# First loads in another order, two more pairs of y tiles for product 5, one query tile for all heads

## Chip, core and metric

The kernel runs on one core of a Trainium2 chip. The metric is the device time of one execution in microseconds (us). The core has five engines that run side by side, each through its own queue in order: PE (matrix products, with its weight loads shown as PEld), ACT, DVE, POOL, and SP, which issues most of the transfers (DMAs). A DMA from SP or POOL goes to the same 16 DMA engines.

## The reference, cut to what matters

Two layers over 1024 latent tokens and 256 context tokens, each of width 1024. Each layer takes a root-mean-square norm of its input, scales and shifts it by a modulation worked out from a conditioning vector, projects it, mixes tokens, and projects back with a gate:

```
def _ada(cvec, w, b):
    m = jax.nn.silu(cvec) @ w + b
    return jnp.split(m.reshape((-1, 1, m.shape[-1])), 3, axis=-1)
...
for l in range(DEPTH):
    shift, scale, gate = _ada(c, w_ada[l], b_ada[l])
    h_lat = _rms(x, norm_w[l]) * (1.0 + scale) + shift
    h_ctx = _rms(ctx, norm_w[l]) * (1.0 + scale_c) + shift_c
    ...   # layer 0: neighbourhood attention beside mLSTM heads; layer 1: 16 HGRN2 heads
    x = x + gate * y_lat
```

Layer 1 (`_c_mixer`) runs for each of 16 heads a gated recurrence in both directions, with query `q`, a decay `f` and key `1 - f` per direction, and ends in an output projection of a 2048 x 1024 weight matrix.

## The kernel before

All arithmetic is float32. A float32 product is split: each operand becomes a high part (`hi`, a cast on ACT, L73) and a low part (`lo`, the difference, on DVE, L74), and three matmuls `hi*hi`, `hi*lo`, `lo*hi` (L131 to L133) make one product. So each weight block and each activation tile is first a raw tile that a DMA fills, and then a pair of tiles.

Tiles come from pools. A tile is asked for under a tag; a tag has a number of buffers, and a further request for the tag gets a buffer when all uses of its earlier tile are over. The order of the instructions on each engine and on SP is not the program's order: a planner lays them out beforehand, by priority (the program's order, with helpers that make some steps urgent and others fillers) and by its own estimate of when each is ready. `issue_after(ins)` puts what a block issues behind `ins` on the queue of `ins`.

Three places matter here.

**The first loads** (from L1293). `load_x` (L1298) loads one 128 x 1024 tile of x and norms it: a square with a sum on ACT (L237), a reciprocal root on POOL (L157, L159), a scaling on DVE (L239). `gate_cols` (L280) loads 272 columns of the first weight matrix, "value weights" (`wvr`), and splits them into `wvh` and `wvl`. `ada` (L186, `ada_rows` L168) loads the modulation weights in eight chunks of 1 MB (`adar`, three buffers), multiplies each on PE (L177), and at the end copies the row (`adarow`, L192), turns it and writes the modulation; its last instruction is `mod_done` (L208). Then, in pairs of tiles, `mod_tr` (L242) transposes x on PE (L251), applies the modulation on ACT and DVE (`ntmp`, L259, L261) and splits the result into `hh` and `hl` (L274, L275); `values_gates` (L292) multiplies these with the value weights. The order of the loads is: two x tiles, value weights, modulation chunks, the other eight x tiles. x tiles have six buffers.

**The heads of layer 1** (L1443). `hg_intra` of a head writes the query tile `gQ` in four pieces (L1038): for the upper half of the tokens (`hf` = 1) and then the lower half, for both directions. Seven levels follow, each a set of small matmuls on PE (L1059, `strip`) and updates of `gQ` and `gK` on DVE (L1106). `hg_scan` (L1119) goes through eight chunks of 128 tokens in rising order; its matmuls at L1138 and L1139 read `gQ`, chunk by chunk, and its state update is `gS` on DVE (L1144). `gQ` has one buffer and is asked for anew in each head.

**The output projection** (from L1463). It is done as seven smaller products over halves of rows and columns. `y_block` (L1504) loads a 128 x 512 tile of the activations and splits it into `yh` and `yl`. For product 5 (weights `w5`, results `m5`), the tiles y of k = 0 to 3 are made early; then k = 4 to 6 (L1614) are loaded, split and used one by one, and k = 7 (`y7`) follows. `later` is a list of weight loads, and `loads()` (L1556) starts the next. `final` (L1548) writes one result tile `og` (four buffers) and adds it into the output in memory with a DMA from POOL; `f2` (L1563) is its use for four tiles just before product 5. `product` (L1589) does products 6, 3 and 4, and `f4` (L1580) writes the last four tiles with plain DMAs from SP.

Of the kernel before, what the change touches and what calls it, by code (L numbers as in the profile page):

```python
# [10 lines left out]
F32 = mybir.dt.float32  # L11
F32R = mybir.dt.float32r
# [7 lines left out]
P = 128  # L20
D = 1024
KD = D // P
LAT = 1024
# [22 lines left out]
class Prog:  # L46
# [980 lines left out]
    def hg_intra(self, h, st, pool):  # L1027
        nc = self.nc
        F, q = st["F"], st["q"]
        K = self.t(pool, [P, 2, LAT], F32, "gK", 1)  # L1030
        nc.vector.tensor_scalar(out=K, in0=F, scalar1=-1.0, scalar2=1.0, op0=ALU.mult, op1=ALU.add)
        Q = self.t(pool, [P, 2, LAT], F32, "gQ", 1)
        ks = [self.t(pool, [P, 512], F32, "gkn", 4) for _ in range(2)]
        for hf in (1, 0):
            s = slice(hf * 512, (hf + 1) * 512)
            nc.vector.tensor_tensor(out=ks[hf], in0=K[:, 0, s], in1=K[:, 1, s], op=ALU.add)
            for d in range(2):
                nc.vector.tensor_tensor(out=Q[:, 1 - d, s], in0=q[hf], in1=F[:, d, s], op=ALU.mult)  # L1038
        hv = dict(Q=Q, K=K, T=F, D=self.t(pool, [P, 8, 64], F32, "gD", 1))
        hv["A"] = self.t(pool, [P, 8, P], F32, "gA", 1)  # L1040
        if h == 0:
            self.t(pool, [P, 16], F32, "pad", 1)
        pa = self.ps("s", [P, 8, 64])
        with self.urgent():
            for c in range(8):
                for b in range(2):
                    o = c % 4 * P + b * 64
                    self.strip(pa[:, c, :], b, ks[c // 4][:, o : o + 64], q[c // 4][:, o : o + 64])
        nc.vector.tensor_tensor(
            out=hv["D"], in0=pa, in1=self.lmask[:, 0, :].unsqueeze(1).to_broadcast([P, 8, 64]), op=ALU.mult  # L1050
        )
        for lev in range(7):
            self.hg_level(hv, lev, pool)
        return hv
# [23 lines left out]
    def hg_level(self, H, lev, pool):  # L1078
        nc = self.nc
        n, h = LAT, 1 << lev  # L1080
        nb = n // (2 * h)
        K, Q, A, D, Tt = H["K"], H["Q"], H["A"], H["D"], H["T"]

        pick = lambda t: _skew(t[:, 0, :].rearrange("p (b s i) -> p b s i", s=2, i=h), 2, n)
        out = self.ps("s", [P, 8, 64])
        with self.urgent():
# [5 lines left out]
            for c in range(8):  # L1092
                for b in range(2):
                    o = c * P + b * 64
                    r = out[:, c, :]
                    if lev < 6:
                        r = r.rearrange("p (b s i) -> p b s i", s=2, i=h)
                        lhsT, rhs = ksel[:, o : o + 64], pick(Q)[:, o // (2 * h) : (o + 64) // (2 * h)]
                    else:
                        lhsT = K[:, b, o : o + 64]  # L1100
                        rhs = Q[:, 1 - b, c * P + (1 - b) * 64 : c * P + (2 - b) * 64]
                    self.strip(r, b, lhsT, rhs)
            for t, o, step in ((Q, n + 1, -n - 1), (K, 1, n - 1)):
                v = bass.AP(t.tensor, t.offset, [list(t.ap[0]), [n + h, 2], [2 * h, nb], [1, h]])
# [106 lines left out]
    def build(self):  # L1211
        tc, nc, a = self.tc, self.nc, self.a
        dma = nc.sync.dma_start
        with ExitStack() as es:
# [78 lines left out]
            with self.pp.phase(ad=1), tc.tile_pool(name="pre", bufs=2) as pool:  # L1293
                self.adab = 3
                self.wide_c(pool)
                xts = {}

                def load_x(tt):  # L1298
                    xts[tt] = self.t(pool, [P, D], F32, "x0", 6)
                    self.last_dma = dma(out=xts[tt], in_=self.xin(tt))  # L1300
                    self.norm(xts[tt], xts[tt], pool)

                for tt in range(2):
                    load_x(tt)
                wv = self.gate_cols(pool)
                with tc.issue_after(self.last_dma.ins):
                    for step in self.ada(0, pool, nc.sync):
                        step()
                mod_pair = lambda tt: self.mod_tr(0, [xts[tt], xts[tt + 1]], tt, pool, self.h_sink(tt * P))
                with tc.issue_after(self.last_dma.ins), tc.issue_after(self.mod_done.ins):  # L1310
                    for tt in range(2, NT):
                        if tt % 2 == 0:
                            mod_pair(tt - 2)
                        load_x(tt)
                x_dma = self.last_dma
                mod_pair(NT - 2)
                self.values_gates(wv)
# [35 lines left out]
            with tc.tile_pool(name="ml", bufs=2) as pool, self.pp.phase(s=2, acc=2):  # L1353
# [22 lines left out]
                yp = wr.enter_context(tc.tile_pool(name="oy", bufs=1, side="right"))  # L1376
# [8 lines left out]
            with tc.tile_pool(name="op0", bufs=2) as op, ExitStack() as wl:  # L1385
# [3 lines left out]
                raws = [yp, 3, "woraw"]  # L1389
# [46 lines left out]
            with l1:  # L1436
                pool = l1.enter_context(tc.tile_pool(name="hg", bufs=2))
# [5 lines left out]
                for h in range(16):  # L1443
# [7 lines left out]
                    if h == 15:  # L1451
                        rh.close()
                        yp = es.enter_context(tc.tile_pool(name="oy", bufs=1, side="right"))
# [19 lines left out]
                def add(out, x, y, op=ALU.add):  # L1473
                    nc.vector.tensor_tensor(out=out, in0=x, in1=y, op=op)
# [21 lines left out]
                for t in range(4):  # L1496
# [4 lines left out]
                    hi, lo = self.out_y(t, 1, y2, yp, 4, ks=((0, 4), (4, 3)))  # L1501
                    self.dense(m2[t], lambda i: hi[i], lambda i: lo[i], w2.h, w2.l, 7, True, False)

                def y_block(src, k, raws):  # L1504
                    yh, yl = [self.t(yp, [P, 512], F32R, "y" + c, 4) for c in "hl"]
                    yr = self.t(*raws)
                    dma(out=yr, in_=src(k))
                    self.split(yh, yl, yr)
                    return yh, yl

                def block_mm(ps, t, y, w, k, n):
                    at = slice(t * P, (t + 1) * P)
                    self.dense(
                        ps, lambda i: y[0][:, at], lambda i: y[1][:, at], lambda i: w.h(k), lambda i: w.l(k),
                        1, k == 0, k == n - 1,
                    )

                later, r16 = [], []
                w5 = block(self.sw[0], _Late(wr * 4, r16), later)
# [3 lines left out]
                w5_dma = self.last_dma  # L1523
                m5 = [self.ps("c", [P, 512]) for _ in range(2)]
                y5 = [y_block(lambda k: self.s5[k], k, (yp, [P, 512], F32, "wraw", self.yraws)) for k in range(4)]
                for k in range(4):
                    for t in range(2):
# [7 lines left out]
            with tc.tile_pool(name="op1", bufs=2) as op, ExitStack() as wl, tc.issue_after(w5_dma.ins):  # L1535
# [6 lines left out]
                for b in range(2):  # L1542
                    g = self.t(op, [P, 512], F32, f"gbc{b}", 1)
# [3 lines left out]

                def final(tt, b, x, y, op_=ALU.add):  # L1548
                    r, c = slice(tt * P, (tt + 1) * P), slice(b * 512, (b + 1) * 512)
                    g = self.t(op, [P, 512], F32, "og", 4)  # L1550
                    add(g, x, y, op_)
                    add(g, g, gates[b], ALU.mult)
                    nc.gpsimd.dma_start(out=a["out"][r, c], in_=g, accum_op=ALU.add)


                def loads():  # L1556
                    for ld in later[:1]:
                        ld()
                    del later[:1]
# [3 lines left out]
                def f2(t, ps):  # L1563
                    final(t, 0, p[:, t, :], ps, ALU.subtract)
# [5 lines left out]
                def f6(t, ps):  # L1570
                    add(u[:, t, :], ps, u[:, t, :])
                    add(p[:, t, :], ps, p[:, t, :])
                    final(4 + t, 1, u[:, t, :], e[:, t, :])
                    add(u[:, t, :], u[:, t, :], gates[0], ALU.mult)
                    add(u[:, t, :], u[:, t, :], rest[:, t, :])

                def f3(t, ps):
                    final(t, 1, p[:, t, :], ps, ALU.subtract)

                def f4(t, ps):  # L1580
                    g = self.t(op, [P, 512], F32, "og", 4)
                    add(g, ps, gates[0], ALU.mult)
                    add(g, g, u[:, t, :])
                    dma(out=a["out"][512 + t * P : 640 + t * P, 0:512], in_=g)
# [16 lines left out]
                            block_mm(ps[t], t, y[k - 6], w, k, 8)  # L1601
                        sink(t, ps[t])

                raws = (op, [P, 512], F32, "yraw", 6)
                for i in range(4):
                    loads()
                for t in range(4):
                    f2(t, m2[t])
                m5 += [self.ps("mm", [P, 512]) for _ in range(2)]
                for k in range(4):  # L1610
                    for t in (2, 3):
                        block_mm(m5[t], t, y5[k], w5, k, 8)
                    loads()
                for k in range(4, 7):  # L1614
                    y = y_block(lambda k: self.s5[k], k, raws)
                    for t in range(4):
                        block_mm(m5[t], t, y, w5, k, 8)
                    loads()
                y7h, y7l = [self.t(op, [P, 512], F32R, "y7" + c, 1) for c in "hl"]
                y7 = self.t(op, [P, 512], F32, "y7", 1)  # L1620
# [7 lines left out]
                product(w6, lambda k: self.s6[k], f6, ("c", "c", "tr", "tr"))  # L1628
                product(w3, lambda k: self.s3[k], f3, ("c", "c", "mm", "mm"))
                product(w4, lambda k: y2[8 + k, :, 512:1024], f4, ("c", "c", "tr", "tr"))  # L1630

    def xin(self, tt):
# [145 lines left out]
```

## Time and profile before

| | |
|---|---|
| time, median of 3 runs (lowest, highest) | 3375.06 us (3374.84, 3375.25) |
| the profiled execution: its time | 3376.8 us |
| the profiled execution: its span in the trace | 3375.0 us |
| PE busy | 3321.0 us (98%), 24982 matmuls |
| DVE, ACT, POOL busy | 2022.1, 1402.1, 661.2 us |
| granted PE clock, mean over the span | 0.996 of full speed |

How to read it: the span is the time from the first to the last instruction in the trace; the run's time holds 1.8 us more around it. A row of the timeline gives the start, the duration, the engine, the line, the operation with its output and inputs, and a count where like instructions were merged; in brackets stands how long the engine had been idle and what ended that. `SPq` and `POOLq` stand for the issue of a DMA by SP or POOL; its data land later. A row of waits gives the sum in us, the number of times, and the longest.

### The profile page before, as it was taken

The numbers are of one execution on the slowest core, as the hardware profiler recorded it, in microseconds if no ns is written. First come the engines' busy times: TensorE is split into PE (matmuls) and PEld (weight loads), VectorE is DVE, ScalarE is ACT, GpSimd is POOL, SyncE is SP. The second block draws the span as 40 slices with busy tenths as digits, with TensorE's granted clock in tenths as the row PEclk, the third lists the DMA queues.
The fourth block names the chain that finished last, engine by engine and source line by source line (L and its number), as shares of the span: only waits on it lengthen the run. The fifth ranks groups of instructions, "written<-read, shape, count | busy, mean of one in ns | idle before, by whom it ended". The sixth has DMA issues, their size and how long they took to land. (4 is left out here: it accounts for less than half of the span.)

```text
span 3375.0 us, 64228 instructions
## 1 busy us (share of the span) xinstructions
PE 3321.0 (98%) x24982; PEld 2940.1 (87%) x24982; DVE 2022.1 (60%) x4791; ACT 1402.1 (42%) x3310; POOL 661.2 (20%) x1059
## 2 busy tenths in 40 slices
PE   6999999999999999999999999999999999999999
PEld 5689999888989888898888999988899999989877
DVE  4437666666655566787656555555555555555557
ACT  5335544555544444454454333333333333333343
POOL 2222222222211112221100111122112222321110
PEclk8999999999999999999999999999999999999999
DMA  6622222232233434444652122122122322222366
GB/s 217 234 85 75 80 77 76 76 91 84 71 90 102 147 119 127 131 137 139 215 170 89 45 70 67 60 65 66 62 66 67 79 60 60 76 73 64 79 178 184
DMA packets 315696, 342.02 MB, mean 101 GB/s; under 512 B 32168, under 2 KB 257128, under 8 KB 313344
## 3 DMA queue, kind: packets, MB, share of 16 engines
q1 hardware_dynamic: 269520, 217.85, 21.9%
q0 software_dynamic: 45872, 120.07, 11.6%
q8 instruction: 197, 3.23, 0.4%
q14 instruction: 107, 0.88, 0.1%
HBM read 253.43 MB, written 84.21 MB: 100 GB/s over the span
## 5 line engine op out<-in xcount | busy, mean ns | idle before, releaser
L131 PE MATMUL mm<-hh,wh 128*128 128x512 f32 (+1 forms) x1600 | 583.2, 365 | 0.7 <-ACT gF L958 0.7
L132 PE MATMUL mm<-hl,wh 128*128 128x512 f32 (+1 forms) x1600 | 582.2, 364 | 0.0
L133 PE MATMUL mm<-hh,wl 128*128 128x512 f32 (+1 forms) x1600 | 581.5, 364 | 0.0
L131 PE MATMUL mm<-wh,hh 128*128 128x256 f32 (+1 forms) x1440 | 445.7, 310 | 2.5 <-DVE graw L300 1.4
L132 PE MATMUL mm<-wl,hh 128*128 128x256 f32 (+1 forms) x1440 | 444.7, 309 | 0.0
L133 PE MATMUL mm<-wh,hl 128*128 128x256 f32 (+1 forms) x1440 | 441.9, 307 | 0.0
L131 PEld LDWEIGHTS mm<-hh,wh 128*128 128x128 f32 x1600 | 301.6, 189 | 48.7 <-issue 2.5
L133 PEld LDWEIGHTS mm<-hh,wl 128*128 128x128 f32 x1600 | 301.4, 188 | 44.6 <-issue 0.2
L132 PEld LDWEIGHTS mm<-hl,wh 128*128 128x128 f32 x1600 | 301.7, 189 | 42.1 <-issue 0.2
L131 PE MATMUL mm<-wzh,hh 128*128 128x256 f32 x1024 | 294.5, 288 | 0.0
L133 PE MATMUL mm<-wzh,hl 128*128 128x256 f32 x1024 | 292.0, 285 | 0.0
L132 PE MATMUL mm<-wzl,hh 128*128 128x256 f32 x1024 | 290.2, 283 | 0.0
L131 PEld LDWEIGHTS mm<-wh,hh 128*128 128x128 f32 x1440 | 271.3, 188 | 21.1 <-ACT ev L322 3.4
L132 PEld LDWEIGHTS mm<-wl,hh 128*128 128x128 f32 x1440 | 271.3, 188 | 12.4 <-issue 0.7
L133 PEld LDWEIGHTS mm<-wh,hl 128*128 128x128 f32 x1440 | 271.2, 188 | 12.0 <-issue 0.5
L74 DVE TENSOR_TENSOR wl<-wraw,wh 128x512 fp32r<-128x512 f32 x240 | 167.7, 703 | 159.1 <-ACT wh L73 157.6
L73 ACT CAST wh<-wraw 128x512 fp32r<-128x512 f32 x240 | 147.2, 618 | 226.6 <-PE mm L132 167.2
L131 PEld LDWEIGHTS mm<-wzh,hh 128*128 128x128 f32 x1024 | 193.4, 189 | 2.5
L132 PEld LDWEIGHTS mm<-wzl,hh 128*128 128x128 f32 x1024 | 193.4, 189 | 1.6
L133 PEld LDWEIGHTS mm<-wzh,hl 128*128 128x128 f32 x1024 | 192.9, 188 | 1.2
L1089 ACT COPY gksel<-gK 128x1024 f32<-128x1024 f32 x96 | 110.8, 1154 | 163.9 <-PE s L1059 118.6
L1106 DVE TENSOR_TENSOR gQ<-gQ,gF 128x1024 f32<-128x1024 f32 x112 | 139.9, 1249 | 45.8 <-PE s L1059 44.8
(467 smaller groups left out, 7411.8 us busy)
## 6 DMA issues: line engine op xcount, KB each, us to landing
wraw<-in_wab_dram SPq DMA_DIRECT2D x108, 256.0 KB
wraw<-in_wc_dram SPq DMA_DIRECT2D x96, 256.0 KB
wraw<-yd SPq DMA_DIRECT2D x92, 256.0 KB
wraw<-in_wc_dram SPq DMA_DIRECT2D x128, 128.0 KB
md<-ev POOLq DMA_DIRECT2D x60, 256.0 KB, 2.7
mloz<-md SPq DMA_DIRECT2D x40, 256.0 KB
s<-gyt POOLq DMA_DIRECT2D x36, 256.0 KB, 4.3
adar<-in_wada_dram SPq DMA_DIRECT2D x8, 1024.0 KB
```

Source lines behind the costliest of these rows:

```text
L73: m = nc.scalar.copy(hi, x)
L74: nc.vector.tensor_tensor(out=lo, in0=x, in1=hi.bitcast(F32), op=ALU.subtract)
L131: mm(ps, lhsT=lh(k), rhs=rh(k), start=(start and k == 0), stop=False)
L132: mm(ps, lhsT=lh(k), rhs=rl(k), start=False, stop=False)
L133: m = mm(ps, lhsT=ll(k), rhs=rh(k), start=False, stop=(stop and k == nk - 1))
L1089: m = nc.scalar.copy(ksel.rearrange("p (b s i) -> p b s i", s=2, i=h), pick(K))
L1106: nc.vector.tensor_tensor(out=v, in0=v, in1=tot, op=ALU.mult)
```

## The change

The modulation chunks are asked for first, then two x tiles, then the value weights; the other x tiles stay last. The tile `gQ` is asked for in head 0 alone, kept, and used by all 16 heads. Two tiles y of product 5 (k = 4 and 5) are made ahead of the first matmuls of that stage, in two new pairs of buffers, and k = 6 is made ahead of the matmuls of k = 4; the six pairs then go round for products 6, 3 and 4 too. The buffers for raw y tiles go from 6 to 4, those for `og` from 4 to 3.

```diff
@@ hg_intra
-        Q = self.t(pool, [P, 2, LAT], F32, "gQ", 1)
+        if h == 0:
+            self.Q = self.t(pool, [P, 2, LAT], F32, "gQ", 1)
+        Q = self.Q
@@ build, first loads
-                for tt in range(2):
-                    load_x(tt)
-                wv = self.gate_cols(pool)
+                for step in self.ada(0, pool, nc.sync):
+                    step()
                 with tc.issue_after(self.last_dma.ins):
-                    for step in self.ada(0, pool, nc.sync):
-                        step()
+                    for tt in range(2):
+                        load_x(tt)
+                with tc.issue_after(self.last_dma.ins):
+                    wv = self.gate_cols(pool)
@@ build, output projection
+                yring = [(yp, 4)] * 4
+
                 def y_block(src, k, raws):
-                    yh, yl = [self.t(yp, [P, 512], F32R, "y" + c, 4) for c in "hl"]
+                    pl, n = yring.pop(0) if yring else (yp, 4)
+                    yring.append((pl, n))
+                    yh, yl = [self.t(pl, [P, 512], F32R, "y" + c, n) for c in "hl"]
...
-                    g = self.t(op, [P, 512], F32, "og", 4)        # in final and in f4
+                    g = self.t(op, [P, 512], F32, "og", 3)
...
-                raws = (op, [P, 512], F32, "yraw", 6)
+                raws = (op, [P, 512], F32, "yraw", 4)
...
                 m5 += [self.ps("mm", [P, 512]) for _ in range(2)]
+                yring[:0] = [(op, 2)] * 2
+                y5 += [y_block(lambda k: self.s5[k], k, raws) for k in (4, 5)]
                 for k in range(4):
                     for t in (2, 3):
                         block_mm(m5[t], t, y5[k], w5, k, 8)
                     loads()
+                y5.append(y_block(lambda k: self.s5[k], 6, raws))
                 for k in range(4, 7):
-                    y = y_block(lambda k: self.s5[k], k, raws)
                     for t in range(4):
-                        block_mm(m5[t], t, y, w5, k, 8)
+                        block_mm(m5[t], t, y5[k], w5, k, 8)
                     loads()
```

More of the change, by code (lines that the diff above doesn't have):

```diff
@@ L1580, in f4 @@
                 def f4(t, ps):
-                    g = self.t(op, [P, 512], F32, "og", 4)
+                    g = self.t(op, [P, 512], F32, "og", 3)
                     add(g, ps, gates[0], ALU.mult)
```

## The prediction

> **What bounds the kernel now.** I read the page's busy times first, then the waits of PE, then the timeline and the busy times in short windows at the three places of the change.
>
> ```profile
> PE 3321.0 (98%) x24982; PEld 2940.1 (87%) x24982; DVE 2022.1 (60%) x4791; ACT 1402.1 (42%) x3310; POOL 661.2 (20%) x1059
> ...
> PE ad L177 <- DMA adar<-in_wada_dram: 20.7, 8, 13.7
> PE s L1059 <- DVE gQ L1038: 7.2, 12, 0.7
> ...
> PE c L131 <- ACT yh L73: 3.7, 1, 3.7
> ```
>
> PE is busy for 3321.0 of 3375.0 us, so nothing moves the end that does not take idle or slow time away from PE. Of the 54 us that are left, 20.7 us are waits for the modulation chunks at the start, 7.2 us are waits for `gQ` in 12 of the heads, and 3.7 us are one wait for a y tile in product 5. The change touches these three. DVE (60%) and ACT (42%) matter only where they are late in one place.
>
> **First loads.** One window row and the timeline of the start:
>
> ```profile
> 0.00:25.00 25.00, 7.35 (x32) 0.83 (x32) 6.26 (x21) 6.31 (x11) 6.42 (x17) 1.00 0.94 334
> ...
> 5.08 1.06 ACT L237 ACTIVATE njk<-x 128x1024 f32<-128x1024 f32 x1 [2.32 <-DMA x<-in_x_dram]
> ...
> 7.28 1.06 ACT L237 ACTIVATE njk<-x 128x1024 f32<-128x1024 f32 x1 [1.05 <-DMA x<-in_x_dram]
> ...
> 11.18 2.28 ACT L73 CAST wvh<-wvr 128x544 fp32r<-128x544 f32 x4 [2.76 <-DMA wvr<-in_wab_dram]
> ...
> 20.88 1.55 PE L177 MATMUL ad<-adar,sc 128*32 128x512 f32 x8 [0.52 <-DMA adar<-in_wada_dram]
> 25.19 1.85 PE L177 MATMUL ad<-adar,sc 128*32 128x512 f32 x8 [2.75 <-DMA adar<-in_wada_dram]
> ...
> 32.55 1.93 PE L177 MATMUL ad<-adar,sc 128*32 128x512 f32 x8 [1.38 <-DMA adar<-in_wada_dram]
> 33.83 1.06 ACT L237 ACTIVATE njk<-x 128x1024 f32<-128x1024 f32 x1 [17.84 <-DMA x<-in_x_dram]
> ...
> 38.87 0.55 ACT L259 ACTIVATE ntmp<-tr,ab 128x256 f32<-128x256 f32 x1
> 39.45 0.41 ACT L274 CAST hh<-ntmp 128x256 fp32r<-128x256 f32 x1
> ...
> 39.91 0.60 PE L131 MATMUL mm<-wvh,hh 128*128 128x272 f32 x1 [0.66 <-ACT hh L274]
> ...
> 40.35 0.87 ACT L274 CAST hh<-ntmp 128x256 fp32r<-128x256 f32 x2
> ```
>
> The DMA engines are full (a share of 0.94 in the first 25 us), so the order decides what is late. Two x tiles and the value weights are ahead of the chunks; the eighth chunk is there at 32.55, and the first product of the values starts 7.36 us later, at 39.91.
>
> After: the first x tile (half a chunk) was there at 5.08; a tile takes half of a chunk's 2.45 us (the last three chunks: 32.55 - 25.19, by 3), so the first chunk lands at 5.08 + 1.25 = 6.3, up to 7.2 with the small loads of POOL beside it. Seven more make 23.5 to 24.4. One interval of before is 4.31 us (20.88 to 25.19), 1.9 too long, for a reason that the trace does not show; if it recurs, 26.3. Then the x tiles, 1.25 each (32.55 to 33.83): 26 to 28.8 for the second. Then the value weights; in before they took from the second x tile's square (7.28) to 11.18, 3.9 us; at the chunks' pace 2.6. So they land at 28.6 to 32.7. Three chains now lead to the first product:
> - the last chunk plus the 7.36 us of before: 30.9 to 33.7;
> - the second x tile, plus its square, `ntmp` and `hh` (1.06 + 0.55 + 0.41 from the rows) and root, scaling and four transposes (together about 3.2, an estimate that takes each at 0.7 to 1.3): 31.2 to 34.0;
> - the value weights plus a quarter of the four casts (2.28 / 4 = 0.57): 29.2 to 33.3.
>
> The latest gives 31.2 to 34.0, that is 6 to 8.7 us sooner, 7.3 in the middle. Part is given back. The casts of the value weights (2.28 us of ACT, and their low parts on DVE) and the squares of the x tiles 2 to 5 (from 33.83 on, four times 1.25 = 5.0), which lay in the shade of the chunks, now stand beside the first pairs of tiles. Cover there:
>
> ```profile
> 40.00:45.00 5.00, 5.00 (x22) 4.72 (x23) 4.55 (x11) 3.29 (x8) 0.73 (x1) 0.50 0.02 3
> 45.00:50.00 5.00, 5.00 (x39) 5.00 (x39) 1.71 (x4) 2.95 (x7) 0.73 (x2) 0.92 0.61 210
> 50.00:55.00 5.00, 3.21 (x27) 2.97 (x26) 4.43 (x13) 4.75 (x14) 1.80 (x4) 1.00 0.26 67
> ```
>
> From 40 to 50 ACT has 10 - 3.29 - 2.95 = 3.8 us free and PE is always busy; from 50 to 55 ACT has 4.75 and PE only 3.21 of 5. So of 7.3 us extra, 3.8 are covered and 3.5 come back. I take -4 us. Bounds: -8.7 with full cover; +1 if ACT alone sets the end of this stage (its first square after the chunks comes no sooner than before, and 2.28 us of casts are added, less idle). What follows is PE-bound up to the end, so whatever is left is kept.
>
> **The query tile.** The four writes of a head:
>
> ```profile
> 2205.13 1.54 PE L1059 MATMUL s<-gQ,gksel 128*64 128x64 f32 x32 [0.62 <-DVE gQ L1038]
> ...
> 2277.80 0.35 DVE L1144 SCALAR_TENSOR_TENSOR gS<-gS,gT,s 128x128 f32<-128x128 f32 x1 [0.86 <-PE acc L1139]
> ...
> 2280.74 0.35 DVE L1144 SCALAR_TENSOR_TENSOR gS<-gS,gT,s 128x128 f32<-128x128 f32 x1 [1.25 <-PE acc L1139]
> ...
> 2290.27 2.50 DVE L1038 TENSOR_TENSOR gQ<-gq,gF 128x512 f32<-128x512 f32 x4 [2.59 <-PE acc L1139]
> ...
> L1038 DVE TENSOR_TENSOR gQ<-gq,gF x64: 679/685/695, 1839.2 to 3170.8; 128x512 f32<-128x512 f32 x64
> ```
>
> All four run in one go after the scan's last read (L1139) and hold PE for 0.62 us. With one kept tile, no write waits for the tile as a whole; it waits for the readers of its own part. That waits here go by parts is seen at 39.45 to 40.35 above: PE reads a part of `hh` before ACT has written others. The lower half's readers are chunks 0 to 3 and end halfway through the scan, where DVE sits idle for 0.86 and 1.25 us before two `gS` updates; two writes (2 x 0.685 = 1.37 us) fit there. So the chain behind the last read falls from 2.50 to about 1.25 us, more than PE's wait. If PE's order stayed as it is, all 7.2 us would go. But the planner puts the strips as soon as it thinks `gQ` ready, with less filler between; it was too early by 0.62 us with four writes, and with two I take half of that. So -3.6 us; bounds 0 and -7.2.
>
> **Product 5.**
>
> ```profile
> 3271.49 1.16 SPq L1507 DMA_DIRECT2D yraw<-s  x2
> 3272.70 2.67 SPq L104 DMA_DIRECT2D woraw<-sw  x2
> ...
> 3276.09 1.71 POOL L1553 DMA_DIRECT2D out_dram<-og  x2 [2.22 <-DVE og L1474]
> ...
> 3279.12 0.68 DVE L1474 TENSOR_TENSOR og<-oacc,c 128x512 f32<-128x512 f32 x1
> ...
> 3285.41 0.39 PE L133 MATMUL mm<-wh,yl 128*128 128x512 f32 x1
> 3288.34 0.62 ACT L73 CAST woh<-woraw 128x512 fp32r<-128x512 f32 x1 [14.35 <-DMA woraw<-sw]
> ...
> 3289.53 0.79 PE L131 MATMUL c<-woh,yh 128*128 128x512 f32 x1 [3.73 <-ACT yh L73]
> ...
> 3290.35 0.62 ACT L73 CAST woh<-woraw 128x512 fp32r<-128x512 f32 x1 [0.87 <-DMA woraw<-sw]
> ...
> 3280.00:3285.00 5.00, 5.00 (x24) 4.14 (x23) 0.53 (x1) 0.00 (x0) 1.17 (x2) 1.00 1.10 262
> 3285.00:3290.00 5.00, 1.27 (x5) 0.81 (x4) 0.69 (x1) 1.14 (x2) 0.00 (x0) 0.85 1.10 267
> 3290.00:3295.00 5.00, 5.00 (x12) 3.51 (x12) 3.92 (x7) 3.21 (x6) 0.00 (x0) 0.50 1.06 386
> ...
> out_dram<-og POOLq DMA_DIRECT2D x4, 256.0 KB, 9.9
> ```
>
> PE ends k = 3 at 3285.6 and waits until 3289.53 for y of k = 4. ACT casts it right behind a weight cast (3288.34) that waited 14.35 us for its own DMA. But the raw y tiles of k = 4 and 5 were asked for at 3271.49, ahead of that weight block (3272.70) on the same queue. At 262 GB/s, shared with POOL's adding writes, 256 KB take 2.0 us, so they landed at about 3284.3 and 3286.3. They stood behind the weights on ACT since `yh` had to wait for the tile of k = 0, which PE used until after 3278. With buffers of their own the two casts can stand first: `yh` at 3285.0 and 3287.0, no wait at k = 4. After the wait the clock is at 0.50 and PE does 12 records in 5 us instead of 24, so another 2.5 us are lost. Both together: 3.73 + 2.5 = 6.2.
>
> What is late next is k = 6. Its DMA is behind the weight block cast at 3290.35, so it lands 0.7 to 2.0 us later (by 386 or 131 GB/s), and is cast by 3291.7 to 3293.0. PE is there after 24 matmuls of 0.23: 3285.6 + 5.5 = 3291.1. It waits for about 0.9 us, too short to matter to the clock: the waits of 1.5 us elsewhere did not lower it.
>
> ```profile
> PE mm L893 <- ACT yh L73: 1.5, 1, 1.5
> ...
> 3175.00:3200.00 25.00, 23.47 (x278) 20.54 (x277) 23.19 (x36) 11.67 (x21) 3.29 (x4) 1.00 0.51 125
> ```
>
> Against it stands `og` with three buffers. The fourth tile of `f2` starts at 3279.12; now it waits for the first one's DMA, issued at 3276.09, with 9.9 us to landing: 3286.0. Its two operations (1.3) hold DVE up to 3287.3, and the low part of y for k = 4, if queued behind, comes at 3288.0, 2 us late. Most of this overlaps the wait at k = 6, and some 1.2 us stay. Whether DVE's order is so I can't see, so I charge half: 6.2 - 0.9 - 0.6 = -4.7 us; bounds 0 and -6.2.
>
> The Trainium skill ("DMA: Bandwidth & Descriptors", section on the anatomy of a DMA on the SWDGE path) gives about 2.0 us plus the bytes at 436 GB/s for such a DMA; by its figures an estimate of 2.6 us for 256 KB. By that, the first `og` would be free at about 3279.5, the smaller number of buffers would cost nothing, and product 5 would bring -5.3. The 9.9 us of this trace speak against it, as adding writes under a full queue are slower.
>
> At the end, `f4` writes four `og` tiles, and the fourth now waits for the first:
>
> ```profile
> 3367.88 4.51 SPq L1584 DMA_DIRECT2D out_dram<-og  x4
> ...
> 3370.62 0.69 DVE L1474 TENSOR_TENSOR og<-tr,gbc 128x512 f32<-128x512 f32 x1
> ```
>
> The last issue ends at 3367.88 + 4.51 = 3372.39, and the span 2.6 us later with all closing steps, so a DMA lands within 2.6 us of its issue; the first by about 3370.8, and the fourth tile is wanted at 3370.62. Cost 0 to 0.2; I take 0. Four raw buffers instead of six are covered by six split pairs instead of four: as many tiles are ahead.
>
> **Sum.** -4 - 3.6 - 4.7 = -12.3 us: span 3362.7, the profiled execution 3376.8 - 12.3 = 3364.5. That execution lies 1.7 above the median; the median becomes 3375.06 - 12.3 = 3362.8, 0.36% faster. About 0.2% (6.8 us) is what a measurement can tell from no change here.
>
> **Rivals.**
> - The kept tile changes nothing in the order (waits do go by the whole tile, or the writes stay together): 0 for 3.6; 3366.4. For it: the upper half is written first in the program.
> - ACT bound at the start: the 4 us are given back in full; 3366.8. For it: ACT's 4.75 of 5 us at 50.
> - The y casts of k = 4 and 5 still stand behind the weight cast on ACT: product 5 keeps its wait and its slow clock; 3367.5. For it: that weight block is asked for earlier in the program.
> - Two of these together: about 3371.
> - Slower: the early writes of `gQ` get in front of `gS` updates on DVE, and PE, at that point out of filler, waits for `gS`. Place: the second half of the scan in 15 heads; price 15 x 2 x 0.685 = 20.6 us; with the other two parts 3375.06 + 20.6 - 8.7 = 3387.0. It decides once DVE's idle before a `gS` is shorter than a write; the 0.86 to 1.25 us of the rows above speak against it.
>
> **How the numbers follow.** Forecast 0.48 (3355 to 3367); kept tile without effect 0.13; start given back 0.12; product 5 as before 0.10; two together 0.08; slower 0.09. The single failures lie near 0.2%, so a third of each counts as no change. Faster 0.48 + 0.23 = 0.71; same 0.12 + 0.08 = 0.20; slower 0.09. The range 3355 to 3372 takes in the forecast with its bounds and all cases but the slower one.
>
> **What would show it.** Right: the eighth chunk's matmuls at 24 to 26.5 and the first value product at 31 to 34; two of the four `gQ` writes between `gS` updates, and PE's wait for L1038 well under 7.2 us; no 3.7 us wait in product 5 and a clock of 1.00 throughout it. Wrong: PE waiting on `gS` (L1144) in the heads; `og` with a long wait on DVE and PE waiting on `yl` behind it; the values stage ending as late as in before although it starts sooner; or a new order of the heads or of the fillers that makes waits where there were none.

## The result, and the profile after

| | before | after |
|---|---|---|
| median of 5 runs (lowest, highest) | 3375.25 us (3374.84, 3380.89) | 3361.22 us (3357.84, 3363.42) |
| the profiled execution: time, span | 3376.8, 3375.0 us | 3363.4, 3361.6 us |

The ratio of after to before is 0.9952 (95% interval 0.9941 to 0.9963): faster by 0.48%. The profiled execution was the slowest of the five. It shows the gain in other places than the sum had it.

The busy times on the page and then rows of the waits of PE, in the kernel after, with one row of before at the end:

```profile
PE 3324.1 (99%) x24982; PEld 2943.7 (88%) x24982; DVE 2032.6 (60%) x4791; ACT 1399.8 (42%) x3310; POOL 658.9 (20%) x1059
```

```profile
PE ad L177 <- DMA adar<-in_wada_dram: 14.9, 8, 6.7
PE tr L251 <- DVE ntmp L261: 3.8, 3, 2.4
...
PE mm L893 <- ACT yh L73: 2.7, 2, 2.4
...
PE c L133 <- DVE yl L74: 0.8, 1, 0.8
```

```profile
PE mm L893 <- ACT yh L73: 3.1, 2, 1.5
```

The waits for `gQ` and for y of k = 4 are gone from the list, and the waits for chunks have shrunk from 20.7 to 14.9 us. The waits of L893 sum to a little less than in before, but not in the same places: of the two waits of 1.53 us in before, the one in the output projection of layer 0 has grown to 2.44 us, and the one at 3197.12 us is gone. (The row of 1.5 us in the prediction is of the last 225 us alone, and is that second one.) To see where the time went, the start time of the same matmul is compared with that in before (us, read from the traces; negative is sooner; the last two columns are experiments told below):

```
place (time in before)                    after   one more execution of after   e4_wf
end of the value products (87.11)         -3.9    -4.0                          -4.4
output projection of layer 0 (1689.46)    -2.8    -3.4                          -3.1
after its wait (1695.50)                  -1.9    -3.9                          -4.8
a few tiles later (1701.59)               -0.3    -3.9                          -5.2
first head (1847.41)                      -0.3    -3.9                          -5.1
last head (3259.41)                       -7.6    -11.5                         -12.0
behind product 5 (3329.51)                -14.3   -18.2                         -18.6
```

So in the profiled execution the start brought 3.9 us, of which 3.6 were lost again up to 1702 us, 2.5 of them near 1691; the heads brought 7.4, and product 5 brought 6.7. Behind the last place a new wait of 0.84 us for a `yl` (L133, at 3330.26 us) stands in after and in its second execution, not in e4_wf; its cause is not shown.

**Start.** Rows of the timeline after, PE, ACT and DVE together, and the last value product of both kernels, before first:

```profile
87.11 0.29 PE L133 MATMUL mm<-wvh,hl 128*128 128x272 f32 x1
```

```profile
6.65 1.93 PE L177 MATMUL ad<-adar,sc 128*32 128x512 f32 x8 [6.65 <-DMA adar<-in_wada_dram]
...
27.26 1.93 PE L177 MATMUL ad<-adar,sc 128*32 128x512 f32 x8 [0.55 <-DMA adar<-in_wada_dram]
...
33.30 2.29 ACT L73 CAST wvh<-wvr 128x544 fp32r<-128x544 f32 x4 [2.11 <-DMA wvr<-in_wab_dram]
...
33.36 0.29 DVE L208 SCALAR_TENSOR_TENSOR ab<-ab,normw 128x8 f32<-128x8 f32 x2
...
33.98 2.63 DVE L74 TENSOR_TENSOR wvl<-wvr,wvh 128x544 fp32r<-128x544 f32 x4 [0.34 <-ACT wvh L73]
...
35.50 0.56 ACT L259 ACTIVATE ntmp<-tr,ab 128x256 f32<-128x256 f32 x1
35.96 1.04 ACT L237 ACTIVATE njk<-x 128x1024 f32<-128x1024 f32 x1
...
36.53 0.54 DVE L261 TENSOR_SCALAR ntmp<-tr,ab 128x256 f32<-128x256 f32 x1
...
37.00 0.39 ACT L274 CAST hh<-ntmp 128x256 fp32r<-128x256 f32 x1
...
37.13 1.12 PE L251 MATMUL tr<-ident,x 128*128 128x128 f32 x4 [2.41 <-DVE ntmp L261]
...
37.90 0.58 PE L131 MATMUL mm<-wvh,hh 128*128 128x272 f32 x1
...
83.20 0.29 PE L133 MATMUL mm<-wvh,hl 128*128 128x272 f32 x1
```

The modulation is ready at 33.65 (33.36 + 0.29). But ACT has begun on the four casts of the value weights at 33.30, and `ntmp` runs only behind them, at 35.50; then a square of a later x tile comes in front of `hh`, which is ready at 37.39. PE waits longer for DVE: DVE makes the four low parts of the value weights from 33.98, its `ntmp` follows at 36.53, and four transposes that stand ahead of the first product on PE wait for it (2.41 us) and start at 37.13. The first value product starts behind them at 37.90.

**Heads.** One head of after, at the second half of its scan:

```profile
2274.81 0.35 DVE L1146 SCALAR_TENSOR_TENSOR gS<-gS,gT,s 128x128 f32<-128x128 f32 x1 [1.13 <-PE acc L1141]
...
2275.26 0.69 DVE L1040 TENSOR_TENSOR gQ<-gq,gF 128x512 f32<-128x512 f32 x1
...
2276.30 0.35 DVE L1146 SCALAR_TENSOR_TENSOR gS<-gS,gT,s 128x128 f32<-128x128 f32 x1 [0.35 <-PE acc L1141]
...
2276.56 0.68 DVE L1040 TENSOR_TENSOR gQ<-gq,gF 128x512 f32<-128x512 f32 x1
...
2284.40 1.29 DVE L1040 TENSOR_TENSOR gQ<-gq,gF 128x512 f32<-128x512 f32 x2 [2.30 <-PE acc L1140]
...
2287.46 1.58 PE L1061 MATMUL s<-gQ,gksel 128*64 128x64 f32 x32
```

Two of the four writes (now L1040) stand between `gS` updates, and the other two are done at 2285.69. The strips that read them come 1.77 us later, and no wait stands before them. The 7.4 us of this stretch hold the wait at 3197.12 us too, so they are not the query tile's alone.

**Product 5.** The requests on SP, the casts on ACT and the windows, after:

```profile
3265.70 1.83 SPq L104 DMA_DIRECT2D woraw<-sw  x2
3267.57 0.58 SPq L1514 DMA_DIRECT2D yraw<-s  x1
```

```profile
3276.85 0.62 ACT L73 CAST yh<-yraw 128x512 fp32r<-128x512 f32 x1 [10.51 <-DMA yraw<-s]
...
3278.85 0.62 ACT L73 CAST yh<-yraw 128x512 fp32r<-128x512 f32 x1 [1.37 <-DMA yraw<-s]
...
3280.86 0.62 ACT L73 CAST woh<-woraw 128x512 fp32r<-128x512 f32 x1 [1.39 <-DMA woraw<-sw]
3282.02 0.62 ACT L73 CAST woh<-woraw 128x512 fp32r<-128x512 f32 x1 [0.54 <-DMA woraw<-sw]
3282.74 0.62 ACT L73 CAST yh<-yraw 128x512 fp32r<-128x512 f32 x1
```

```profile
3280.00:3285.00 5.00, 5.00 (x22) 3.67 (x22) 3.12 (x6) 2.76 (x5) 0.00 (x0) 1.00 1.04 390
3285.00:3290.00 5.00, 5.00 (x23) 4.09 (x22) 5.00 (x9) 4.19 (x8) 0.84 (x1) 1.00 0.64 174
```

The two y tiles (k = 4 and 5) are cast ahead of the weights, and the third (k = 6) behind them; PE is busy for 5 of 5 us at a clock of 1.00, where before had 1.27 of 5 and then a clock of 0.50.

### The profile page after: what moved, and what is told of

Same layout as the page of the kernel before. It is cut to its first block, busy times and chain, and to the rows that moved or that the text cites. A ratio compares the mean times of both kernels' runs of the same rounds, so it can differ in the third digit from the quotient of the medians.

```text
span 3361.6 us, 64235 instructions
## 1 busy us (share of the span) xinstructions
PE 3324.1 (99%) x24982; PEld 2943.7 (88%) x24982; DVE 2032.6 (60%) x4791; ACT 1399.8 (42%) x3310; POOL 658.9 (20%) x1059
## 5 line engine op out<-in xcount | busy, mean ns | idle before, releaser
L133 PE MATMUL mm<-hh,wl 128*128 128x512 f32 (+1 forms) x1600 | 580.4, 363 | 0.0
L133 PE MATMUL mm<-wh,hl 128*128 128x256 f32 (+1 forms) x1440 | 441.9, 307 | 0.0
L133 PEld LDWEIGHTS mm<-hh,wl 128*128 128x128 f32 x1600 | 301.5, 188 | 43.8 <-issue 0.2
L133 PE MATMUL mm<-wzh,hl 128*128 128x256 f32 x1024 | 291.6, 285 | 0.0
L133 PEld LDWEIGHTS mm<-wh,hl 128*128 128x128 f32 x1440 | 271.3, 188 | 12.0 <-issue 0.5
L133 PEld LDWEIGHTS mm<-wzh,hl 128*128 128x128 f32 x1024 | 193.3, 189 | 1.6
```

The lines of the kernel that those rows point to most:

```text
L133: m = mm(ps, lhsT=ll(k), rhs=rh(k), start=False, stop=(stop and k == nk - 1))
```

## The experiments

Times are medians of 5 to 11 runs. The kernels were timed in three groups of four, each beside before on one chip: before took 3375.34 us beside e1 to e4, 3376.56 beside e5 to e8 and 3375.61 beside e9 to e12. e4_wf (3358.56), with which later kernels are compared, is of the first group.

### Each part alone

```diff
  e1_loads: only the order of the first loads (chunks, two x tiles, value weights)
  e2_gq:    only
-        Q = self.t(pool, [P, 2, LAT], F32, "gQ", 1)
+        if h == 0:
+            self.Q = self.t(pool, [P, 2, LAT], F32, "gQ", 1)
  e3_p5:    only the edits of the output projection (pairs, requests, og 3, yraw 4)
```

> Only the order of the first loads is changed; everything else is as before. Theory (the loss near 1690 us belongs to the new start): 3.7 us are won by 100 us into the span and about 3 of them are lost again between 1600 and 1850 us, where the matmuls of the output projection wait 2.8 us instead of 1.9 and the clock halves for 3.4 us; total 3371 to 3373 against 3375.3. Rival (the loss comes with the other two parts, or is a chance of one execution): the whole 3.7 us stay, total 3371 to 3372, and no clock drop at 1695 us. Told apart by the offset of the heads' first strips against before: -0.3 or -3.7 us.

> Only the kept query tile. Theory (the tile is waited for part by part once it is kept, so that two of the four writes run inside the scan and the other two end before the strips need them): the whole wait of 7.2 us over the 16 heads goes and nothing takes its place, 3367.9 to 3368.5 us. Rival (the forecast of the prediction: half of the wait stays): 3371.5 us.

> Only the product 5 part: two more pairs of y tiles, requests ahead of the matmuls, three og and four yraw buffers. Theory (wait of 3.7 us and the half clock behind it both go, the third og buffer costs nothing because the fourth og is put behind the casts): 5.8 to 6.2 us less, 3369.0 to 3369.5. Rival (the prediction's term: 0.9 us of wait at k = 6 and 0.6 us for og stay): 4.7 us less, 3370.6.

Measured: 3372.49 (ratio 0.9989, 0.9980 to 0.9998), 3369.35 (0.9983, 0.9974 to 0.9992) and 3368.27 (0.9979, 0.9970 to 0.9988). That is 2.9, 6.0 and 7.1 us, together 15.9; the whole change brought 14.0 above and 16.2 in its second measurement below, which the intervals do not tell apart, so the parts add up. In the traces the heads of e2_gq bring 7.7 us (the wait at 3197 us is gone there too) and product 5 of e3_p5 brings 6.7. For e2_gq the theory was right that the whole wait goes, and its time lies between the two theories; e3_p5 came out a little better than its theory. In e1_loads the start won 4.9 us, 3.7 of it was lost by 1702 us, and the clock dropped there. That agreed with the theory that the loss belongs to the new start; e11_again below shows that it need not come with it.

### The query tile: is it the halves?

```diff
  e6_whole (on e4_wf)
         Q = self.Q
+        if h:
+            nc.vector.memset(Q.rearrange("p d (c f) -> p d c f", f=64)[:, :, :, 0:1], 0.0)
```

> The kernel of e4_wf, with a fill of every 64th column of the kept query tile at the head of each head's writes, so that the first write needs the whole tile free and all four writes stand behind the last update of the scan. Theory (what the kept tile brings is that its halves are waited for separately): the wait of 7.2 us is back, and the fill adds 0.1 to 0.2 us in each of 15 heads, 3366 to 3369. Rival (the tile kept under one name changes the order of the heads' work, and the writes by halves are incidental): 3359 to 3361, the fill's own time at most.

Measured: 3367.69 us, 9.1 more than e4_wf and 9.7 more than e7_pairs, which was timed beside it. The waits of PE in e6_whole:

```profile
PE s L1063 <- DVE gQ L1042: 9.4, 12, 0.9
```

The tile is kept, but as soon as something must wait for all of it, the wait is back: 9.4 us against 7.2 in before, with 15 fills of 0.085 us ahead of the writes, as the theory had it. So it is the separate wait for each half that wins the time.

### Product 5: the pairs or the place of the requests, and the og buffers

```diff
  e7_pairs (on e4_wf)
-                y5 += [y_block(lambda k: self.s5[k], k, raws) for k in (4, 5)]
...
-                y5.append(y_block(lambda k: self.s5[k], 6, raws))
                 for k in range(4, 7):
+                    y5.append(y_block(lambda k: self.s5[k], k, raws))
  e9_og2 (on e4_wf), in final and f4
-                    g = self.t(op, [P, 512], F32, "og", 3)
+                    g = self.t(op, [P, 512], F32, "og", 2)
```

> The kernel of e4_wf, with the two more pairs of y tiles kept, and the three tiles of product 5 requested inside its loop as before the change. Theory (the pairs are what frees the tiles; the place of the requests follows from them): under 1 us from e4_wf, 3358 to 3359.6. Rival (the requests ahead of the matmuls are what brings the casts forward): the wait of 3.7 us at k = 4 and the half clock are back in part, 3361 to 3364.

> The kernel of e4_wf with two og buffers in place of three (four before the change). Theory (the last og tiles are put behind the casts of the y tiles and stall nothing on TensorE's path): within 0.5 us of e4_wf, 3358 to 3359. Rival (the prediction's step: each og buffer less makes a result wait for an adding write of about 10 us, and VectorE waits with it ahead of casts): two waits of up to 3 us become visible in product 5 or in the products behind it, 3361 or more.

Measured: 3357.96 and 3359.03 us, against 3358.56 of e4_wf. Neither differs, as both theories had it, and in the traces PE waits 0.2 and 0.3 us for `yh` in product 5, where before had 3.7. The pairs do it without the early place of the requests in the program; with a free pair the planner puts the requests early by itself. And even two `og` buffers cost nothing that shows. The place of the late `og` on DVE explains it for after:

```profile
3279.50 0.69 DVE L74 TENSOR_TENSOR yl<-yraw,yh 128x512 fp32r<-128x512 f32 x1 [1.30 <-ACT yh L73]
...
3285.36 0.68 DVE L1477 TENSOR_TENSOR og<-oacc,c 128x512 f32<-128x512 f32 x1
...
3286.56 0.69 DVE L1477 TENSOR_TENSOR og<-og,gbc 128x512 f32<-128x512 f32 x1
```

The fourth `og`, which ran at 3279.12 in before, is now at 3285.36, behind the low part of y at 3279.50. The planner did not leave it in front to hold DVE. That this place is why the buffers cost nothing is read from the order, not tried.

### The wait at 1691 us

The first matmul behind the wait (timeline) and the windows there (the clock is third from the end), for before, for after, for a second execution of after (e11_again) and for e1_loads:

```profile
1695.50 0.50 PE L893 MATMUL mm<-woh,yh 128*128 128x512 f32 x1 [1.53 <-ACT yh L73]
```

```profile
1695.00:1700.00 5.00, 4.50 (x18) 3.41 (x19) 2.70 (x5) 2.04 (x4) 0.00 (x0) 1.00 0.60 183
```

```profile
1693.63 0.50 PE L893 MATMUL mm<-woh,yh 128*128 128x512 f32 x1 [2.44 <-ACT yh L73]
```

```profile
1695.00:1700.00 5.00, 5.00 (x17) 3.93 (x16) 2.54 (x5) 1.63 (x3) 0.00 (x0) 0.66 0.68 197
```

```profile
1691.63 0.50 PE L893 MATMUL mm<-woh,yh 128*128 128x512 f32 x1 [1.08 <-ACT yh L73]
```

```profile
1695.00:1700.00 5.00, 5.00 (x24) 4.14 (x23) 3.23 (x6) 2.81 (x6) 0.74 (x2) 1.00 0.50 140
```

```profile
1692.69 0.50 PE L893 MATMUL mm<-woh,yh 128*128 128x512 f32 x1 [1.99 <-ACT yh L73]
```

```profile
1690.00:1695.00 5.00, 3.02 (x11) 1.83 (x10) 2.08 (x3) 1.85 (x3) 0.00 (x0) 0.90 0.68 222
1695.00:1700.00 5.00, 5.00 (x19) 3.98 (x18) 2.58 (x4) 2.51 (x5) 0.02 (x1) 0.76 0.64 184
```

The wait was 1.53, 2.44, 1.08 and 1.99 us. (The expectations count it by PE's weight loads: 1.97, 2.88, 1.52 and 2.42.) Behind 1.08 and 1.53 the clock stays at 1.00; behind 1.99 and 2.44 it drops. In e2_gq and e3_p5, with the old start, the wait was 1.06 and 1.46 us and the clock stayed. The Trainium skill ("TensorE: Matmul & The Clock Gate", the part on the clock gate) lets the clock fall after about 3.4 us of idle in a window that runs on its own; these two waits were shorter and it fell, and the measurement decides. What is waited for stands on SP and ACT in after:

```profile
1685.39 0.51 SPq L104 DMA_DIRECT2D wraw<-in_wc_dram  x1
1686.00 1.01 SPq L874 DMA_DIRECT2D wraw<-yd  x2
```

```profile
1692.15 0.62 ACT L73 CAST wh<-wraw 128x512 fp32r<-128x512 f32 x1 [8.70 <-DMA wraw<-in_wc_dram]
1692.96 1.35 ACT L73 CAST yh<-wraw 128x512 fp32r<-128x512 f32 x2 [0.20 <-DMA wraw<-yd]
```

The y tiles of the next row are asked for behind a block of the heads' first weights (`wf`, from `in_wc_dram`), which the heads use only behind this whole stage, and are cast behind it: ACT waits for `wf` up to 1692.15, and `yh` follows at 1692.96. e4_wf and e10_bwf move that request, after and before:

```diff
  e4_wf on the kernel after, e10_bwf on the kernel before
-                wf = [self.wring([a["wc"][:, 2048 : 2048 + P]], P), None]
                 for tt in [8, 9, 4, 5, 6, 7, 0, 1, 2, 3]:
...
                     self.mod_tr(1, [xn], tt, op, self.h_sink(tt * P, P))
+                    if tt == 5:
+                        wf = [self.wring([a["wc"][:, 2048 : 2048 + P]], P), None]
```

> The changed kernel with one line moved: the first weights of the heads (wf) are requested behind the fourth tile of the output projection and not ahead of its first. Theory (the wait near 1691 us is for y tiles whose raw buffers and queue places are held by these weights): the wait of 2.4 us and the half clock at 1695 us go, 3 us less than the changed kernel, about 3358. Rival (the y tiles wait for the broadcasts of the gates and for the bandwidth in any order): the wait stays, 3361, or the weights come late for the first strips and the total grows by 1 to 2 us.

> The kernel before, with the request of wf moved behind the fourth tile, as in e4_wf, and nothing else. Theory (this wait stood in the kernel before too, 1.9 us without a drop of the clock): 2.1 us less than before, 3373 to 3374, no wait over 1 us near 1691. Rival (the wait is a matter of the new start): no change.

> The changed kernel once more, unaltered, beside the others on one chip. Theory (with the new start the wait near 1691 us is over 2 us and the clock halves behind it each time): again a wait of 2.4 to 2.9 us, a clock of 0.6 to 0.9 in one of the slices from 1690 to 1700 us, and 2.5 to 3.5 us more than e4_wf. Rival (the length of the wait differs by execution): a wait of 1.5 to 2 us and no drop in this one.

Measured: e4_wf 3358.56, e10_bwf 3373.12 (2.5 less than before; ratio 0.9991, 0.9982 to 1.0000), e11_again 3359.41 us (3358.82 to 3359.79). In e4_wf and e10_bwf the wait is gone. The window of e4_wf:

```profile
1690.00:1695.00 5.00, 5.00 (x23) 4.13 (x22) 3.19 (x5) 2.00 (x4) 0.00 (x0) 1.00 0.75 247
```

e11_again decides for its rival: the same program waited 1.08 us here and kept its clock, and had 3.9 of the 4.0 us from the start left at the heads. So the loss in the first profile need not come with the new start. From one execution to the other the y tiles landed 2.0 us sooner (their cast is at 1690.95 in place of 1692.96), 1.4 of it because they were asked for sooner (1684.57 in place of 1686.00), and PE came 0.6 us sooner. Of the six waits the two longest let the clock drop, which added 1.6 us in the first profile. Whether the new start makes a long wait more likely stays open: with it the wait was 1.08, 1.99 and 2.44 us, with the old start 1.06, 1.46 and 1.53. The 2.5 us of e10_bwf are at the edge of what its interval tells from nothing. By the medians e4_wf is 0.9 to 2.7 us faster than the change, which the intervals do not tell apart (0.9950, 0.9938 to 0.9963, against 0.9950, 0.9936 to 0.9963); that it beats it is not shown.

### The start

```diff
  e8_oldstart (on e4_wf): the first loads as in before
  e5_pool (on e4_wf), in gate_cols, k pairs 2 and 3
-            self.split(hi[:, k : k + 2, :], lo[:, k : k + 2, :], raw[:, k : k + 2, :])
+                self.nc.gpsimd.tensor_copy(h, x)       # h, x: these two k of hi and raw
+                self.nc.vector.tensor_tensor(out=lo[:, k : k + 2, :], in0=x, in1=h.bitcast(F32), op=ALU.subtract)
  e12_split (on e4_wf), in gate_cols; each load then takes the k blocks k to k + m alone
-        for c, n, c0 in ((0, 256, 2 * D), (256, 16, 9 * D)):
+        for k, m, c, n, c0 in [(0, KD, 256, 16, 9 * D)] + [(k, 2, 0, 256, 2 * D) for k in range(0, KD, 2)]:
```

> The kernel of e4_wf with the old order of the first loads (two x tiles, value weights, modulation weights). Theory (the new order is worth 3 to 4 us at 100 us, and e1_loads showed 2.9 of them because the wait near 1691 us took the rest): 3361.5 to 3362.6, and no wait over 2 us near 1691. Rival (part of the order's gain is lost in any case at a later bound): 3359 to 3360.5.

> The kernel of e4_wf, with the last two of the four casts of the value weights (wvh, k pairs 2 and 3) on GpSimd and not on ScalarE. Theory (behind the loads the start waits for ScalarE, which is busy without a gap from 35 to 50 us): 4.6 us of casts leave it, the last value product ends 2 to 4 us sooner, 3355 to 3357 against 3358.6. Rival (VectorE or the square of x tiles end last anyway, or the cast on GpSimd is slow and the later products wait for it): same or up to 4 us later, 3358 to 3363.

> The kernel of e4_wf with the load of the value weights cut into four, one for each pair of k blocks. Theory (the first casts on ScalarE wait for the whole tile to land, and its quarters are waited for separately): the first cast starts at about 31 us in place of 33.3, and up to 2 us are won, 3356.5 to 3358. Rival (modulation and x tiles end last, the casts have slack; or the order of the first writes on ScalarE gets worse): 3358 to 3360.

Measured: e8_oldstart 3360.34, e5_pool 3358.48, e12_split 3360.22 us. e8_oldstart is 1.8 us over e4_wf and 2.4 over e7_pairs, which was timed beside it, inside its rival's range and under its theory's 3 to 4. The end of the value products tells more than the medians: over the five traces with the old order it is at 85.42 to 87.11 (mean 86.1), over the seven with the new order alone at 82.19 to 83.84 (mean 82.95). The order of the loads is worth 3.1 us there, with the first profile of before the latest of its kind. At the matmul of 1689.46 us, still ahead of the wait, the same traces lie 2.7 us apart.

The theories of e5_pool (2 to 4 us sooner) and of e12_split (up to 2) failed; e12_split lies 0.2 us above its rival's range too. Its casts did start sooner, but the first product came only 0.1 us sooner, at 37.79:

```profile
31.28 2.63 ACT L73 CAST wvh<-wvr 128x544 fp32r<-128x544 f32 x4
34.59 1.06 ACT L237 ACTIVATE njk<-x 128x1024 f32<-128x1024 f32 x1 [0.68 <-DMA x<-in_x_dram]
...
35.83 0.56 ACT L259 ACTIVATE ntmp<-tr,ab 128x256 f32<-128x256 f32 x1
```

```profile
35.57 0.23 DVE L208 SCALAR_TENSOR_TENSOR ab<-ab,normw 128x8 f32<-128x8 f32 x2
```

`ntmp` stands at 35.83 in place of 35.50. DVE had put the low parts of the value weights in front of the modulation, which was ready at 35.80 and not at 33.65; the values end at 83.11 (after 83.20). In e5_pool two of the four casts left ACT, 1.1 us and not the 4.6 of the expectation (all four take 2.29). `ntmp` is 1.2 us sooner there, at 34.33, the first product 0.9 us sooner, at 37.02 (PE again waits for DVE's `ntmp` before it), and the values end at 82.37, within the range above. So 1 us less on ACT ahead of the first product brings nothing that can be told at the end of this stage. What sets that end is not settled. The window of after shows ACT (14.74) and DVE (13.18) busy for nearly all of the 15 us that follow, and the work of the pairs of tiles passes through both:

```profile
35.00:50.00 15.00, 12.31 (x76) 11.80 (x77) 13.18 (x29) 14.74 (x36) 6.25 (x13) 0.72 0.34 128
```

## Why the prediction was right, and where it was not

It gave 3362.8 us (3355 to 3372); measured 3361.22. The total came out of one term too large and two too small; the profiled execution also had a loss that was not foreseen. The three places were the right ones, and the closeness of the total is in part luck.

- **First loads: -4 predicted, -2.9 by time alone and -3.1 at the end of the value products.** The step that failed is the first product at 31.2 to 34.0, so 7.3 us sooner; it came at 37.90, 2.0 sooner. The eighth chunk's matmuls came at 27.26, 0.8 us behind the range, as the chunks took 2.94 us each ((27.26 - 6.65) / 7) and not 2.45. From there to the first product it was 10.64 us and not the 7.36 of before: the modulation was ready after 6.39 us (5.75 in before), ACT's `ntmp` started 1.85 us behind it (0.57), as the casts of the value weights came first, and the first product 2.40 us behind that (1.04), as DVE's low parts of the value weights held back its `ntmp` and the transposes that wait for it. The sum put casts and low parts beside the pairs behind the first product; they stood in front of it. So 5.3 of the 7.3 us went ahead of the first product, and the values then took 45.3 us from the first product to the last, in place of 47.2. That 3.9 us were left in this profile, as forecast, is luck in part. What sets the end of the stage is open, since taking two casts off ACT (e5_pool) or starting them sooner (e12_split) won nothing that can be told.
- **Query tile: -3.6 predicted, -6.0 by time and -7.7 in the trace of e2_gq.** The mechanism was right: halves waited for separately, two writes in the scan, 1.29 us behind it. The step that failed is that the planner would take half of it back by putting the strips earlier: they come 1.77 us behind the last write. All 7.2 us of waits went, the upper bound; the 7.7 of the trace hold the lost wait at 3197 us too.
- **Product 5: -4.7 predicted, -7.1 by time and -6.7 in the trace.** The casts at 3285.0 and 3287.0, in the time of before, came at 3276.85 and 3278.85, where this stage starts 7.6 sooner: 3284.5 and 3286.5. What failed are the two deductions. There is no wait at k = 6: its request still stands behind both weight blocks on SP (3267.57 behind 3265.70), but these were cast 1.16 us apart (2.01 in before), and it was cast 0.72 us behind the second, the low end of the 0.7 to 2.0 of the sum. The cast ended at 3283.36, which is 3291.0 in the time of before, just when PE came (3291.1 in the sum). A likely reason, not tested, is that the fourth adding write was not yet under way (issued at 3287.54, behind these casts; in before at 3280.82, ahead of them). And the `og` buffers cost nothing. That the Trainium skill's figure ("DMA: Bandwidth & Descriptors", the anatomy of a DMA on the SWDGE path) also gave no cost for `og` is no proof for it: the planner moved the tile, and in after three of these writes took 9.7 us (median) from issue to landing, near the 9.9 of before and far from 2.6.
- **"What follows is PE-bound up to the end, so whatever is left is kept."** Not in the profiled execution: 3.6 of 3.9 us went by 1702 us, 1.1 ahead of 1690 us and 2.5 through a wait of the kernel before that was 0.9 us longer here (2.44 against 1.53) and the half clock behind it, 1.6 us. In this execution that loss hid that the terms were too small. Whether it also lies behind the 14.0 us of the medians, against the 15.9 of the three parts and the 16.2 of e11_again, is not shown: the median run of after has no trace and a mean clock of 1.000, and the intervals do not tell these apart.
- **The slower rival** (early writes in front of `gS`, 3387) did not come: no wait for `gS` stands in the list, and the idle before a `gS` that follows a write is still 0.35 us.

## What to carry to other kernels

A tile kept under one name can be waited for in parts, where a tile asked for anew is waited for as a whole; look for writes whose readers end at different times. When a load is moved, count what its consumers then put in front of the first use on their engines (here casts on ACT and low parts on DVE), in addition to the landing. A wait of 1 to 2.5 us for a DMA differs between executions and sometimes drops the clock behind it, so the profile of one execution can hide or invent a few microseconds.

## What the hardware showed that was not expected

A lower clock at the start cost nothing that can be told. The same start ran in e9_og2 at a clock of 1.00 from 20 to 50 us, and in after at 0.66:

```profile
20.00:50.00 30.00, 22.10 (x120) 15.57 (x117) 16.35 (x39) 19.09 (x43) 7.77 (x17) 1.00 0.67 247
```

```profile
20.00:50.00 30.00, 21.17 (x116) 15.60 (x117) 16.40 (x39) 19.10 (x43) 7.78 (x17) 0.66 0.68 250
```

The value products ended at 82.83 and 83.20. Over the seven traces with the new order alone they ended at 83.2 on average where the clock was 1.00 there (three), and at 82.8 where it was 0.60 to 0.83 (four). PE was busy for 21 to 22 of these 30 us; that a slow clock only fills its idle time is likely, not shown. The same drop at 1695 us, where PE had no other wait, cost 1.6 us at once.
